# A gated convolution block on one core: five of TensorE's convolution tiles as three half-length filters, with their surroundings reordered

## The chip, the core and the metric

The kernel runs on one core of one Trainium2 chip. Time is device microseconds from start to end of one execution. The kernel before takes 1095.86 us, the median of 3 runs (1095.54 to 1095.91). Besides the times there is one profiled execution, from which all rows in this document are taken unless another kernel is named. Engines are PE (TensorE), PEld (its weight loads), DVE (VectorE), ACT (ScalarE), POOL (GpSimd) and SP (SyncE, which issues nearly all DMAs). L802 is line 802 of the kernel.

## What is computed

One layer of a decoder on 256 tokens of width 2048, in float32. A condition vector gives six modulation vectors; the mixer is a gated causal depthwise convolution with 31 taps, between two matrix products and followed by a layer norm; then comes an MLP of width 8192.

```python
mod = silu(c) @ mod_w + mod_b
sh1, sc1, g1, sh2, sc2, g2 = split(mod, 6)
h = rms_norm(x, norm1_g) * (1 + sc1) + sh1
a, gt = split(h @ conv_w_in + conv_b_in, 2)
u = a * sigmoid(gt)
u = depthwise_conv(u, dw_w, left padding 30) + dw_b     # 31 taps, each channel by itself
y = silu(layer_norm(u, ln_g, ln_b)) @ w_out + b_out
x = x + (1 + g1) * y
h = rms_norm(x, norm2_g) * (1 + sc2) + sh2
x = x + (1 + g2) * (square(relu(h @ mlp_w1)) @ mlp_w2)
```

## The kernel before

Activations lie with channels on partitions: 2048 channels are 16 tiles of 128 partitions x 256 tokens. Weights come as 1 MB blocks through seven "raw" buffers. Each is split into a high part (ScalarE, L209) and a low part (L213, on VectorE or GpSimd), and products are made of three reduced-precision matmuls.

The program is a list of jobs. Jobs 0 to 7 (the first half of the input product) run together at the start, at the pace of the DMAs. The loop then takes job 8 to 15 ("in", one tile of `a` and `gt` each), eight "out" jobs, and 64 "up" and "down" jobs. An in-job has 64 or 96 matmuls (L238, L239; job 15 merged, L234 to L236). Its result is added up on VectorE (L537, `evac`) and gated: ScalarE takes the sigmoid (L817), VectorE multiplies (L819, `gate`) and so writes u of the tile. The results of in-jobs and of TensorE's convolution tiles go in turn through two PSUM buffers called "mm"; the gate reads the buffer in place.

The 16 convolution tiles are shared out:

- Eight on VectorE (2, 3, 4, 5, 6, 8, 11, 13): 31 multiply-adds each ("taps", L670 to L676), two tiles interleaved, and a join (L679). `ADVANCE[n]` says how many taps are put into the program behind the gate of job n; the rest comes in job 14.
- One on GpSimd (tile 7): ScalarE multiplies (L703), GpSimd sums (L705), seven taps a job, `POOL_TAPS`.
- Seven on TensorE (0, 1, 9, 10, 12, 14, 15), `pe_conv`, L802. Partitions carry 32 channels x 4 neighbouring taps: `copy_wide` makes from u four shifted copies of 32 partitions, for each of four groups of channels (16 copies of 32x284, on ScalarE, L779; for tile 15 half on VectorE, L777). `make_diag` spreads the taps over diagonals of 32x32 (GpSimd, L787). A tile is then 8 matmuls for each of four groups, of 32 output columns and 256 tokens, side by side in the array. `CONV_AT` puts tile 0 behind job 9, 1 behind 10, 9 behind 11, 10 behind 12, 12 behind 14, 14 behind 15; `COPY_AT` puts the copies a job ahead. The result is evacuated by ScalarE (L810), or by VectorE for tiles 14 and 15.

Between jobs TensorE also computes modulation rows (`mod_chunk`, L328, 16 to 20 matmuls of 32 columns; `mod_finish`, L375, folds a finished group) and sums for the layer norm. `find_shift` (L428) takes the mean of two finished tiles; it is subtracted from every tile (`add_shift`, L741) so that the sums of squares stay exact. `stats` (L480 on ScalarE, L747 on TensorE) sums finished tiles and their squares by 32 columns: tiles 0 to 3 and 4 to 7 in job 14's turn, 8 to 11 behind tile 14. One modulation column ("col", a dot product of 2048 elements on VectorE, `mod_col`, L408) is taken in job 15's turn. Tile 15 is convolved last; then the layer norm follows.

What sets the order: each engine runs its instructions in order; a scheduler orders them by priority when the program is built, `urgent()` raises one, and `tc.issue_after` keeps one instruction behind another. Engines wait for each other by semaphores, and for a buffer until its last reader is done.

## Time and profile before

| | |
|---|---|
| median of 3 runs | 1095.86 us |
| profiled execution, its time | 1095.74 us |
| its span, first to last instruction | 1093.8 us |
| granted TensorE clock, mean | 0.997 |
| start, paced by DMAs | 0 to 123 us |
| in-jobs 8 to 15 with convolution | 137 to 283 us |
| layer norm, out-jobs, MLP | 283 to 1093 us |

A profile row gives the engine, line and operation, the tile written and the tiles read (out<-in), shapes and count. In groups, the figures are busy us and mean ns, then idle time of the engine just before and who ended it. In timelines and the chain, they are start and duration in us; operations of an engine overlap at their edges, so the step from one start to the next is some 0.09 us shorter than a duration. "x64" means that so many in a row were merged. In the row by stretches each engine has its busy us and instruction count.

### The profile page before, as it was taken

The page shows a single profiled execution, that of the slowest core. Times are in us where ns is not written, and L with a number is a line of the kernel's source. Part 1 is how long each engine was busy: PE and PEld are TensorE (multiplying, and loading weights), DVE is VectorE, ACT ScalarE, POOL GpSimd, SP SyncE. Part 2 cuts the span into 40 slices and gives each one's busy share as a digit, 9 for nine tenths or more (in the row PEclk, how much of TensorE's full clock was granted, in tenths as well). Part 3 has the DMA queues.
Part 4 walks back from the last instruction along what each step waited for, and adds up shares of the span by engine and source line. Part 5 has one row for each costly group of instructions (what it writes and reads, how often), then busy time and mean ns, then how long its engine had stood idle before and what let it go on. Part 6 is the DMA issues. An engine that isn't in the chain of part 4 may idle for free.

```text
span 1093.8 us, 15366 instructions
## 1 busy us (share of the span) xinstructions
PE 1075.9 (98%) x5970; PEld 889.9 (81%) x5970; DVE 748.5 (68%) x1019; ACT 520.1 (48%) x706; POOL 217.4 (20%) x149
## 2 busy tenths in 40 slices
PE   6999999999999999999999999999999999999998
PEld 3877876768699988888888888888888888888887
DVE  5777889997667877768855677545566665565653
ACT  4111398677675686444444444333444333444431
POOL 0000169989599251000000000000000000000000
PEclk8999999999999999999999999999999999999999
DMA  9999997995999967899977889657888877788611
GB/s 384 420 420 420 416 416 288 391 371 216 375 393 403 372 248 253 265 296 341 419 266 206 253 258 318 235 144 290 248 242 237 225 214 214 230 251 235 214 66 39
DMA packets 142314, 314.20 MB, mean 287 GB/s; under 512 B 87585, under 2 KB 105505, under 8 KB 107297
## 3 DMA queue, kind: packets, MB, share of 16 engines
q1 hardware_dynamic: 142096, 313.10, 81.6%
q8 instruction: 47, 0.77, 0.3%
q14 instruction: 25, 0.20, 0.0%
q10 hardware_dynamic: 146, 0.13, 0.0%
HBM read 301.13 MB, written 12.07 MB: 286 GB/s over the span
## 4 chain that ended last, share of the span: by engine, by line
PE 86%; DMA 10%; DVE 3%; ACT 1%; issue 0%; SPq 0%; ACTq 0%
PE mm L276 20%; PE mm L275 20%; PE mm L277 20%; DMA raw<-mod_c 9%; PE mm L238 6%; PE mm L239 3%; PE acc L235 2%; PE acc L234 2%; PE acc L236 2%; PE row L328 2%; PE mm L802 2%; DVE raw L408 1%; DMA x<-x 1%; DVE wide L777 1%; PE mm L234 0%; PE mm L236 0%
## 5 line engine op out<-in xcount | busy, mean ns | idle before, releaser
L209 ACT ACTIVATE hi<-raw 128x1024 fp32r<-128x1024 f32 x320 | 335.7, 1058 | 357.4 <-PE mm L277 328.3
L213 DVE TENSOR_TENSOR lo<-raw,hi 128x1024 fp32r<-128x1024 f32 x257 | 312.3, 1220 | 182.7 <-ACT hi L209 180.9
L276 PE MATMUL mm<-lo,u 128*128 128x512 f32 x496 | 193.0, 389 | 0.0
L275 PE MATMUL mm<-hi,u 128*128 128x512 f32 x496 | 193.0, 389 | 0.0
L277 PE MATMUL mm<-hi,u 128*128 128x512 f32 x496 | 192.9, 389 | 0.0
L277 PE MATMUL mm<-hi,hl 128*128 128x512 f32 x480 | 186.7, 389 | 0.0
L276 PE MATMUL mm<-lo,hl 128*128 128x512 f32 x480 | 186.7, 389 | 0.0
L275 PE MATMUL mm<-hi,hl 128*128 128x512 f32 x480 | 186.7, 389 | 0.0
L213 POOL TENSOR_TENSOR lo<-raw,hi 128x1024 fp32r<-128x1024 f32 x63 | 156.2, 2506 | 33.4 <-ACT hi L209 33.3
L408 DVE SCALAR_TENSOR_TENSOR raw<-raw,cond 128x2048 f32<-128x2048 f32 x50 | 117.8, 2358 | 40.5 <-DMA raw<-mod_c 40.5
L277 PEld LDWEIGHTS mm<-hi,u 128*128 128x128 f32 x496 | 93.1, 188 | 19.3
L276 PEld LDWEIGHTS mm<-lo,u 128*128 128x128 f32 x496 | 93.1, 188 | 19.1
L275 PEld LDWEIGHTS mm<-hi,u 128*128 128x128 f32 x496 | 93.1, 188 | 19.0
L277 PEld LDWEIGHTS mm<-hi,hl 128*128 128x128 f32 x480 | 90.1, 188 | 18.7
L275 PEld LDWEIGHTS mm<-hi,hl 128*128 128x128 f32 x480 | 90.1, 188 | 18.7
L276 PEld LDWEIGHTS mm<-lo,hl 128*128 128x128 f32 x480 | 90.1, 188 | 18.7
L676 DVE SCALAR_TENSOR_TENSOR acc<-u,v,acc 128x256 f32<-128x256 f32 x224 | 95.8, 488 | 1.8
L238 PE MATMUL mm<-hl,hi 128*128 128x512 f32 x224 | 80.3, 402 | 0.0
L580 PE MATMUL mm<-two,first 128*128 128x256 f32 x240 | 56.7, 390 | 8.9 <-ACT two L638 8.9
L234 PE MATMUL acc<-hl,hi 128*128 128x256 f32 x224 | 63.4, 283 | 0.0
L235 PE MATMUL acc<-hl,hi 128*128 128x256 f32 x224 | 63.4, 283 | 0.0
L236 PE MATMUL acc<-hl,lo 128*128 128x256 f32 x224 | 63.4, 283 | 0.0
(218 smaller groups left out, 1286.8 us busy)
## 6 DMA issues: line engine op xcount, KB each, us to landing
raw<-w SPq DMA_DIRECT2D x128, 1024.0 KB, 5.5
raw<-mod_c SPq DMA_DIRECT2D x62, 1024.0 KB, 11.3
raw<-mod_r SPq DMA_DIRECT2D x32, 1024.0 KB, 8.7
raw<-w_in SPq DMA_DIRECT2D x16, 1024.0 KB, 11.2
raw<-w_out SPq DMA_DIRECT2D x16, 1024.0 KB, 7.9
first<-w_first SPq DMA_DIRECT2D x15, 1024.0 KB, 19.8
flat<-two SPq DMA_DIRECT2D x30, 256.0 KB, 2.6
two<-flat SPq DMA_DIRECT2D x120, 64.0 KB, 4.4
```

Of the source, the lines that this page charges most:

```text
L209: state["w_hi"] = nc.scalar.activation(hi, w[:, ks, :], AF.Copy).ins
L213: end = by.tensor_tensor(lo, w[:, ks, :], hi.bitcast(F32), op=ALU.subtract)
L234: nc.tensor.matmul(out_p, w, m[:, 0:T], start=begin, stop=False)
L235: nc.tensor.matmul(out_p, w, m[:, T : 2 * T], start=False, stop=False)
L236: state["mm_end"] = nc.tensor.matmul(out_p, lo[:, k % HALF, :], m[:, 0:T], start=False, stop=end)
L238: nc.tensor.matmul(p[:, c, :], hi[:, k % HALF, :], m, start=(k == 0), stop=(k == KT - 1))
L275: nc.tensor.matmul(p, p_hi, hi, start=begin, stop=False)
L276: nc.tensor.matmul(p, p_hi, lo, start=False, stop=False)
L277: nc.tensor.matmul(p, p_lo, hi, start=False, stop=end)
L408: nc.vector.scalar_tensor_tensor(w, w, 1.0, cb, op0=ALU.mult, op1=ALU.mult, accum_out=acc)
L580: step = nc.tensor.matmul(held[n][:, c, :], w[:, 2 * n + c, :], h, start=k == 0 and c == 0, stop=k == KT - 1, skip_group_check=True)
L676: nc.vector.scalar_tensor_tensor(out, s, w, acc, op0=ALU.mult, op1=ALU.add)
```

## The change

Tiles 0, 1, 9, 10 and 12 (`FAST`) are convolved otherwise; 14 and 15 (`PLAIN`) as before. With even and odd samples of u and even and odd taps, both halves of the output come from three filters of 16 taps on 128 samples: the even taps on the sum of two neighbouring phases (needed by both), and two differences of taps, each on one phase. So:

- `copy_phases`: the 16 copies per tile now hold the two phases one after the other, 32 x (2 x 140), from every second sample of u.
- `add_phases`: VectorE adds the two phases (128x560), a buffer "added" of its own, behind the gate of the job before.
- `fast_conv`: 3 parts x 4 x 4 groups = 48 matmuls of 32 columns and 128 samples in place of 32 of 256. ScalarE evacuates the shared part with the bias (128x128), VectorE adds it to the two others into every second sample of the tile.
- `make_diag`: 48 in place of 32 diagonals for these tiles, one buffer in place of two (tile 14 has its own). Once ahead of the loop GpSimd subtracts the filters from each other (128x5x32).

Around it: `find_shift` moves from behind tile 1 to between job 11's matmuls and tile 9 and its two column sums stand together. `mod_finish` of an in-job waits for the end of that job's matmuls, and is not called again behind the rows. `stats` of tiles 0 to 3 moves behind the rows of job 13, that of 4 to 7 behind tile 12. The modulation column comes ahead of the last shift in the program, and that shift (tile 12) reads the SBUF copy. `ADVANCE` falls by 18 taps in jobs 9 to 13. For tile 15 VectorE makes six of the copies, ScalarE ten. u has eight buffers in place of nine, "rest" one in place of two, the partial products of tile 7 use mu and mu2, and the padding on the right side is smaller.

As built, the matmuls of jobs 9 to 14 have nothing between them; VectorE's stream holds add_phases one to four taps behind the gates of tiles 8 to 11 and 13; GpSimd's holds the diag of tiles 1, 9 and 10 between the sums of tile 7; and the modulation column stands between the gates of tiles 13 and 14.

```diff
 FIRST = 4
-PE_TILES = (0, 1, 9, 10, 12, 14, 15)
 CONV_AT = {9: (0,), 10: (1,), 11: (9,), 12: (10,), 14: (12,), 15: (14,)}
+FAST = (0, 1, 9, 10, 12)
+PLAIN = (14, 15)
+HT = T // 2
+PHASE = HT + 12
 POOL_TILE = 7
 POOL_TAPS = {8: 2, 9: 7, 10: 7, 11: 7, 12: 7}
-ADVANCE = {7: 41, 8: 10, 9: 44, 10: 47, 11: 39, 12: 34, 13: 24, 14: 99}
+ADVANCE = {7: 41, 8: 10, 9: 42, 10: 43, 11: 36, 12: 32, 13: 17, 14: 99}
 SHIFT = 2
+SHIFT_AT = 9
 COPY_AT = {8: 0, 9: 1, 10: 9, 11: 10, 13: 12}
-PADDING = 752
+PADDING = 672
 UNSHIFTED = 7
...
     nc.scalar.dma_start(v[:, 0:soon], vec[:, 0:soon])
-    dwq_sb = const.tile([P, 32 * len(PE_TILES)], F32, name="dwq_sb")
+    dwq_sb = const.tile([P, 48 * len(FAST) + 32 * len(PLAIN)], F32, name="dwq_sb")
 
...
         for i, s in enumerate(tiles):
-            nc.tensor.matmul(
-                p, ones, s, start=first and i == 0, stop=last and i == len(tiles) - 1
-            )
+            end = nc.tensor.matmul(p, ones, s, start=first and i == 0, stop=last and i == len(tiles) - 1).ins
+        return end
 
...
     last_mm(hl[HALF - 1][:, 1, :], ((hi_a, lo_a), (hi_b, lo_b)))
+    f = dwq_sb[:, 0 : 48 * len(FAST)].rearrange("p (t a b) -> p t a b", t=len(FAST), a=3)
+    with urgent():
+        nc.gpsimd.tensor_tensor(
+            f[:, :, 1:3, :], f[:, :, 1:3, :], f[:, :, 0:1, :].to_broadcast([P, len(FAST), 2, 16]), op=ALU.subtract
+        )
     start_scope.__exit__(None, None, None)
...
 
+    mu, mu2 = [cvp.tile([P, T], F32, name=name) for name in ("mu", "mu2")]
+
     def cv(k):
...
     u = {}
-    ubufs += [cp.tile([P, PAD + T + 1], F32, name=f"u{i}") for i in range(EARLY_U, 9)]
+    ubufs += [cp.tile([P, PAD + T + 1], F32, name=f"u{i}") for i in range(EARLY_U, 8)]
     for ub in ubufs[EARLY_U:]:
...
         acc = ps.tile([P, 2, T], F32, name="acc", bufs=2)
-        rest = cp.tile([P, T], F32, name="rest", bufs=2)
+        rest = cp.tile([P, T], F32, name="rest", bufs=1)
         for j in range(TAPS):
...
 
-    on_dve = [ct for ct in range(KT) if ct not in PE_TILES and ct != POOL_TILE]
+    on_dve = [ct for ct in range(KT) if ct not in FAST + PLAIN and ct != POOL_TILE]
     taken_taps = iter(range(1, TAPS))
...
         slots = [cvs[3][:, m, :] for m in range(4)] + [cv(11)]
-        slots += [cp.tile([P, T], F32, name="part", bufs=2) for _ in range(n - len(slots))]
+        slots += [mu, mu2]
         with urgent(), tc.issue_after(state["sg"].ins), tc.issue_after(state["pool"]):
...
         p = state["small"][:, 0:T]
-        column_sum(p, [cv(k) for k in range(SHIFT)])
+        end = column_sum(p, [cv(k) for k in range(SHIFT)])
         state["shift"] = cp.tile([P, T], F32, name="shift", bufs=1)
...
             nc.scalar.activation(dst, p, AF.Copy, scale=-1.0 / (SHIFT * P))
+        return end
 
...
 
+    added = {}
+
+    def copy_phases(ct):
+        wides[ct] = cp.tile([P, 4, 2, PHASE], F32, name="wide", bufs=2)
+        for q in range(4):
+            for g in range(4):
+                src = u[ct][32 * g : 32 * g + 32, 2 * q : 2 * q + 2 * PHASE].rearrange("p (x s) -> p s x", s=2)
+                nc.scalar.activation(wides[ct][32 * q : 32 * q + 32, g, :, :], src, AF.Copy)
+
+    def add_phases(ct):
+        added[ct] = cp.tile([P, 4, PHASE], F32, name="added", bufs=1)
+        nc.vector.tensor_tensor(added[ct], wides[ct][:, :, 0, :], wides[ct][:, :, 1, :], op=ALU.add)
+
     def copy_wide(ct, both=True):
+        if ct in FAST:
+            return copy_phases(ct)
         wides[ct] = cp.tile([P, 4, T + 28], F32, name="wide", bufs=2)
...
                 src = u[ct][32 * g : 32 * g + 32, q : q + T + 28]
-                if both and g % 2:
+                if both and g % 2 and q:
                     nc.vector.tensor_copy(dst, src)
...
     def make_diag(ct):
-        diags[ct] = cp.tile([P, 32, 32], F32, name="diag", bufs=2)
-        at = PE_TILES.index(ct)
+        fast = ct in FAST
+        n, at = (48, 48 * FAST.index(ct)) if fast else (32, 48 * len(FAST) + 32 * PLAIN.index(ct))
+        name = "diag14" if ct == PLAIN[0] else "diag"
+        whole = cp.tile([P, 32 if ct == PLAIN[0] else 48, 32], F32, name=name, bufs=1)
+        diags[ct] = whole[:, 0:n, :]
         with tc.issue_after(state["pool"]):
...
                 diags[ct],
-                col("same", 0, 32)[:, None, :].to_broadcast([P, 32, 32]),
-                dwq_sb[:, 32 * at : 32 * at + 32][:, :, None].to_broadcast([P, 32, 32]),
+                col("same", 0, 32)[:, None, :].to_broadcast([P, n, 32]),
+                dwq_sb[:, at : at + n][:, :, None].to_broadcast([P, n, 32]),
                 op=ALU.mult,
+            )
+
+    def fast_conv(ct):
+        wide, diag, total = wides.pop(ct), diags.pop(ct), added.pop(ct)
+        p = ps.tile([P, 2, 2 * T], F32, name="mm", bufs=2)[:, 0, :]
+        for part in (2, 1, 0):
+            for m in range(4):
+                for g in range(4):
+                    src = total[:, g, :] if part == 0 else wide[:, g, part % 2, :]
+                    at = HT * part
+                    state["conv_end"] = nc.tensor.matmul(
+                        p[32 * g : 32 * g + 32, at : at + HT], diag[:, 16 * part + 4 * g + m, :],
+                        src[:, 4 * m : 4 * m + HT], start=m == 0, stop=m == 3,
+                    )
+        with urgent():
+            shared = two()[:, 0, 0:HT]
+            nc.scalar.activation(shared, p[:, 0:HT], AF.Identity, bias=col("dwb", ct))
+            nc.vector.tensor_tensor(
+                cv(ct).rearrange("p (x s) -> p s x", s=2), p[:, HT : 3 * HT].rearrange("p (s x) -> p s x", s=2),
+                shared[:, None, :].to_broadcast([P, 2, HT]), op=ALU.add,
             )
...
     def mix(ct):
-        pe_conv(ct)
-        if ct == SHIFT - 1:
-            find_shift()
+        with tc.issue_after(find_shift()) if ct == SHIFT_AT else ExitStack():
+            (fast_conv if ct in FAST else pe_conv)(ct)
 
...
             splits(jobs[n + 1])
+        for ct in CONV_AT.get(n, ()):
+            if ct in FAST:
+                with tc.issue_after(state["gated"]):
+                    add_phases(ct)
         if n in COPY_AT:
...
                 mm(p, c, job + (c,), hl, merged=kind == "out")
-        mod_finish()
+        with tc.issue_after(state["mm_end"].ins) if kind == "in" else ExitStack():
+            mod_finish()
         if kind == "in":
...
             if n == KT - 1:
-                state["e_end"] = add_shift(cvs[3][:, 0:1, :], 1)
                 for key, w in taken:
                     mod_col(key[1], w)
+                state["e_end"] = nc.vector.tensor_tensor(cv(12), cv(12), state["shift"], op=ALU.add).ins
             for ct in CONV_AT.get(n, ()):
...
                     state["rows_end"] = state["row_end"].ins
-            if rows:
-                mod_finish()
             with tc.issue_after(state["gated"]):
                 advance(ADVANCE.get(n, 0))
-            if n == KT - 2:
-                with tc.issue_after(state["mm_end"].ins):
-                    for b in range(2):
-                        stats(b)
+            if n in (KT - 3, KT - 2):
+                with tc.issue_after(state["row_end" if n == KT - 3 else "conv_end"].ins):
+                    stats(n - KT + 3)
+                state["rows_end"] = state["stats_end"].ins
             if n < KT - 1:
...
             with urgent():
-                mu = cvp.tile([P, T], F32, name="mu")
-                mu2 = cvp.tile([P, T], F32, name="mu2")
                 factor = ps.tile([P, 512], F32, name="small", bufs=1)
...
     taps[:TAPS] = np.asarray(conv_dw_w)[0]
-    dwq = taps.reshape(8, 4, KT, 4, 32).transpose(1, 4, 2, 3, 0).reshape(P, KT, 32)[:, list(PE_TILES)]
-    dwq = np.ascontiguousarray(dwq.reshape(P, 32 * len(PE_TILES)))
+    def in_groups(a, n):
+        return a.reshape(n, 4, KT, 4, 32).transpose(1, 4, 2, 3, 0).reshape(P, KT, 4 * n)
+
+    even, odd = taps[0::2], taps[1::2]
+    ahead = np.concatenate([np.zeros((1, D), np.float32), odd[:-1]])
+    fast = np.stack([in_groups(a, 4)[:, list(FAST)] for a in (even, odd, ahead)], axis=2).reshape(P, -1)
+    dwq = np.concatenate([fast, in_groups(taps, 8)[:, list(PLAIN)].reshape(P, -1)], axis=1)
+    dwq = np.ascontiguousarray(dwq)
     pick = np.tile(np.eye(32, 4, dtype=np.float32), (4, 1))
```

## The prediction

> **What bounds the kernel now.** First TensorE's forty slices on the page, a group of its costliest (used below: one modulation column on VectorE, 2358 ns), and one stretch of the convolution stage in busy us by engine (TensorE, its weight loads, VectorE, ScalarE, GpSimd), clock and DMA.
>
> ```profile
> PE   6999999999999999999999999999999999999998
> ...
> L408 DVE SCALAR_TENSOR_TENSOR raw<-raw,cond 128x2048 f32<-128x2048 f32 x50 | 117.8, 2358 | 40.5 <-DMA raw<-mod_c 40.5
> ...
> 200.00:220.00 20.00, 20.00 (x177) 13.79 (x176) 20.00 (x55) 9.32 (x16) 19.53 (x14) 1.00 1.00 405
> ```
>
> TensorE is never idle for a slice after the start, at a clock of 1.00, so whatever it saves in the convolution stage shortens the run, unless it then waits. But in that stage VectorE is at 20.00 of 20 us and GpSimd at 19.53. The chain of waits in order of time shows TensorE's side: the in-jobs, and between them the convolution tiles (64 instructions each) and row matmuls.
>
> ```profile
> 169.16 0.43 PE mm L238
> 170.42 0.24 PE mm L238
> ...
> 180.67 3.59 PE mm L802 x64
> 184.26 0.63 PE small L428 x2
> 184.89 3.57 PE row L328 x32
> 188.46 0.43 PE mm L238
> ...
> 208.27 0.43 PE mm L238
> ...
> 227.57 0.43 PE mm L238
> ...
> 252.44 3.59 PE mm L802 x64
> 256.02 1.28 PE small L747 x20
> 257.31 0.32 PE mm L234
> ...
> 278.79 3.76 PE acc L802 x61
> ...
> 392.80 3.63 PE row L343 x128
> ```
>
> In-jobs 10, 11, 12, 13 and 15 begin at 169.1, 188.5, 208.3, 227.6 and 257.3. A job's matmuls take 11.5 us (169.16 to 180.67). Two "mm" buffers alternate between jobs and tiles, so each of these starts needs the gate of the job before (L819) to have read its buffer. Hence VectorE's timeline, the gates of tiles 9 to 15 and what stands around them:
>
> ```profile
> 167.31 0.48 DVE L819 SCALAR_TENSOR_TENSOR u<-mm,v,two 128x256 f32<-128x256 f32 x1 [0.54 <-ACT two L817]
> 167.71 10.27 DVE L676 SCALAR_TENSOR_TENSOR acc<-u,v,acc 128x256 f32<-128x256 f32 x26
> ...
> 184.54 0.69 DVE L537 TENSOR_TENSOR mm<-mm,two 128x512 f32<-128x512 f32 x1
> ...
> 186.05 0.48 DVE L819 SCALAR_TENSOR_TENSOR u<-mm,v,two 128x256 f32<-128x256 f32 x1
> ...
> 205.37 0.49 DVE L819 SCALAR_TENSOR_TENSOR u<-mm,v,two 128x256 f32<-128x256 f32 x1
> ...
> 224.89 0.48 DVE L819 SCALAR_TENSOR_TENSOR u<-mm,v,two 128x256 f32<-128x256 f32 x1
> ...
> 242.68 0.48 DVE L819 SCALAR_TENSOR_TENSOR u<-mm,v,two 128x256 f32<-128x256 f32 x1 [0.55 <-ACT two L817]
> ...
> 255.51 0.48 DVE L819 SCALAR_TENSOR_TENSOR u<-mm,v,two 128x256 f32<-128x256 f32 x1
> 255.90 5.73 DVE L676 SCALAR_TENSOR_TENSOR acc<-u,v,acc 128x256 f32<-128x256 f32 x11
> ...
> 266.73 3.52 DVE L408 SCALAR_TENSOR_TENSOR raw<-raw,cond 128x2048 f32<-128x2048 f32 x1
> ...
> 271.55 0.48 DVE L819 SCALAR_TENSOR_TENSOR u<-mm,v,two 128x256 f32<-128x256 f32 x1 [1.30 <-ACT two L817]
> 272.07 7.00 DVE L777 COPY wide<-u 32x284 f32<-32x284 f32 x8
> ```
>
> Job 10's matmuls end at 180.67, yet VectorE takes up the result at 184.54: it is 3.9 us behind, on conv taps. Its gates end only 1.3 (167.8 against 169.1), 2.0, 2.4, 2.3 and 1.4 us before TensorE starts the next job. TensorE is the bound by about 2 us; VectorE is next.
>
> **What TensorE saves.** The changed tile is 48 matmuls of 128 columns, 96 instructions. The row with their form (128x32 weights, 128 columns) is L343 above: 3.63/128 = 28.4 ns. So 96 x 28.4 = 2.72 us against 3.59: 0.87 each, 4.35 for five. [...]
>
> Regrouping: job 11 runs from 188.46 with one column-sum matmul in its middle; two beside each other and beside a tile save one re-entry, the difference of a first matmul's 0.43 and the usual 0.24. Three such places, with mod_finish and the sums inside job 15: 0.2 each, 0.6. All told TensorE needs 5.0 us less. The copies for tile 15 (272.07) shrink from eight on VectorE to six.
>
> **What VectorE gets.** Per fast tile two operations: add_phases, 128x560, two SBUF inputs; and the closing add, 128x256 from PSUM, 0.34 from one start to the next (below, as L1030 by size). ADVANCE takes taps out ahead of gates (2, 4, 3, 2, 7 of them), at 10.27/26 = 0.395 a tap between two tiles, 5.73/11 = 0.52 when one tile runs alone. Nothing removes a tap: they move to the last job. The price of add_phases hangs on GpSimd:
>
> ```profile
> 326.11 2.36 DVE L224 TENSOR_TENSOR u<-two,u 128x512 fp32r<-128x512 f32 x1 [0.65 <-ACT u L221]
> 330.88 0.69 DVE L1030 TENSOR_TENSOR x<-acc,x 128x512 f32<-128x512 f32 x1 [2.41 <-ACT acc L1029]
> 346.23 2.63 DVE L224 TENSOR_TENSOR u<-two,u 128x512 fp32r<-128x512 f32 x1 [4.02 <-ACT u L221]
> 367.44 0.72 DVE L224 TENSOR_TENSOR u<-two,u 128x512 fp32r<-128x512 f32 x1
> ...
> 323.14 7.59 POOL L213 TENSOR_TENSOR lo<-raw,hi 128x1024 fp32r<-128x1024 f32 x3
> 343.53 4.78 POOL L213 TENSOR_TENSOR lo<-raw,hi 128x1024 fp32r<-128x1024 f32 x2
> ```
>
> L224 takes 0.72 us while GpSimd is idle (367.44), but begun at 346.23 it ends at 348.86, 0.55 after GpSimd's subtraction (343.53 + 4.78 = 348.31). An operation with two SBUF inputs waits until GpSimd's current one is over, then runs; one with a PSUM input does not (L1030, 0.69). So add_phases costs 0.7 (0.64 step x 560/512) if GpSimd is free, and 0.7 + 2.4 if it has just begun a subtraction. GpSimd's own round:
>
> ```profile
> 179.72 9.45 POOL L213 TENSOR_TENSOR lo<-raw,hi 128x1024 fp32r<-128x1024 f32 x4
> 189.14 1.91 POOL L787 TENSOR_TENSOR diag<-v,dwq_sb 128x1024 f32<-128x1024 f32 x1
> 191.01 4.00 POOL L705 TENSOR_TENSOR cv<-cv,cv 128x256 f32<-128x256 f32 x5
> ...
> 213.58 9.50 POOL L213 TENSOR_TENSOR lo<-raw,hi 128x1024 fp32r<-128x1024 f32 x4
> ...
> 245.18 9.46 POOL L213 TENSOR_TENSOR lo<-raw,hi 128x1024 fp32r<-128x1024 f32 x4
> ```
>
> Four subtractions of 2.36, a diag that grows with 48/32 from 1.91 to 2.87, seven sums of 0.8: 17.9 us, always busy. The mean rest of the current operation is (9.45 x 1.18 + 2.87 x 1.43 + 5.6 x 0.4)/17.9 = 0.98. I take add_phases at 1.65, between its ends 0.7 and 3.1. The round itself grows by 1 us and by the adds it lets in, but job 13's weights begin at 213.58 and are wanted at 227.6: 14 us of cover, of which three diags and three adds use 5. The subtraction of filters ahead of the loop (160 elements) is under one 0.8 us sum, in GpSimd's wait for the first weights; its dwq load, 152 for 112 KB, is 0.1 us at the 405 GB/s above.
>
> ScalarE: sixteen phase copies per tile in place of sixteen wide ones, and a 128-column evacuation for a 256-column one.
>
> ```profile
> 154.44 7.19 ACT L779 ACTIVATE wide<-u 32x284 f32<-32x284 f32 x16
> ```
>
> No row shows every second element read. I take 0.45 a copy (7.19/16); the other end is double, 0.9. [...] With eight instead of nine u buffers, gates 8 and 9 reuse tiles 0 and 1 after their copies, the later of which end at 161.6 for a gate at 167.3: nothing; without that 5.7 us cover the gate would wait. The second buffers of diag and rest are gone: a diag is written in GpSimd's turn, 9.45 us of subtractions after the tile before it began, and a tile takes 2.7; rest is written and joined on one engine in order. Nothing either.
>
> **The gates, worked forward** in the built order of instructions, starts of L819. Gate 9 waits on ScalarE in both: 167.8. To gate 10, before 18.74 (186.05 - 167.31): four taps fewer (-1.57), a lone tap now paired (-0.13), +1.65 +0.34: 19.0, so 186.85. TensorE, 0.87 earlier at job 10, would need 19.3 (169.16 to 188.46) less 0.87 for the tile and 0.63 for the sums that leave this place, and be ready at 186.1; the gate ends at 187.25. To gate 11, before 19.32: five taps fewer (-1.96), a join traded for a closing add, +1.65: 205.85; TensorE, begun at 187.3, needs the 19.8 of before (188.46 to 208.27) less 0.87 and 0.2 and is ready at 206.0; the gate ends at 206.25. To gate 12, before 19.52: one tap and a pairing less (-0.5), a join more, half the shift-add left for later (-0.9), +2.0: 20.4, so 226.25, ending 226.65, with TensorE ready at 206.3 + 19.3 - 1.07 = 224.5. Job 13 begins at 226.7, before 227.57: of four tiles' 3.5 us and 0.4 of regrouping 0.9 is left. Gate 13 waits for ScalarE's copies at the closing add: 243.8, which delays nobody, since job 14 needs no gate.
>
> To gate 14 the modulation column (L408) now comes first: it was behind cv 12 at 266.73. Before 12.83; the add 1.65, the column 2.36 + 0.95 for GpSimd, four taps fewer (-2.0), 0.5 of idle time filled: 15.3, so 259.1. Its raw buffer comes free some 17 us sooner, and one load behind it on SP's queue goes earlier; no load is waited for there. Queued behind the column are gate 14 and so job 15: TensorE is ready at 226.7 + 29.7 (227.57 to 257.31) - 0.87 + 0.77 (twelve of its sums' 1.28/20 moved in) = 256.3 and begins at 259.5, 2.2 later than before. Job 15, rid of those twelve and a re-entry (-1.0), ends 1.2 late. Between gates 14 and 15 stand 22 lone taps (11.4), a closing add that waits for sixteen copies and one evacuation on ScalarE (259.5 + 16 x 0.45 + 0.4 = 267.1), and a shift with two SBUF inputs (0.34 + 1.0): gate 15 at 274.8, not 271.55. Then a tap and six copies, which take turns with GpSimd's last subtractions as the eight did: 275.2 + 6/8 of 7.00 = 280.4, not 278.79. Tile 15 starts there: **+1.6 us**. Behind it the code is the same and TensorE full, so this stays.
>
> The profiled run took 1095.74 around its span of 1093.8; the median is 1095.86. Sum: 1095.74 + 1.6 = 1097.3; on the median 1097.5. I say **1097.4**.
>
> **Rivals.** (a) The gates come in time and TensorE's 5.0 us stay: 1090.8. For it: every matmul is certain. Against it: even without the waits of add 10, add 12 and the column (0.95 each) gate 14 starts at 256.2, gate 15 (1.0 less for the shift) at 270.9, and ten copies on ScalarE end at 275.9 or later: tile 15 is some 2.8 us early, not 5. 12%. (b) GpSimd becomes the bound. Job 15 uses its second column half first, whose weights are the third subtraction of the round at 245.18: ready at 252.3, wanted at 257.3, 5 us of cover. Five diags at 1.0, five adds at 0.7 and the column at 2.36 that now falls into this round make 10.9 us, less GpSimd's idle time between rounds; from 5 us on job 15 waits for GpSimd, and with the 22 taps behind it, +3 to +5: 1099.8. For it: 19.53 of 20; against: TensorE is itself held back by the gates. 26%. (c) The short filters do not shorten: 57 ns per instruction as in L802, 5.5 us a tile, +9: 1105; or ScalarE's copies cost double, 7 us a job on an engine that all gates pass through: +8. L343 speaks against the first. 5%.
>
> **How the numbers follow.** Forecast (VectorE's gates pace, the gain is given back) 57%, its own range -2.8 (all adds 0.7) to +3.5 (half of them at 3.1, GpSimd's subtraction just begun): 1093.1 to 1099.4. A measurement tells 0.2% from no change, 2.2 us: 1093.7 to 1098.1. Of the forecast 6 points lie below, 43 within, 8 above; (a) is faster, (b) slower but for 2, (c) slower: 18%, 45%, 37%. Leaving out (a)'s better half, (c) and the tails, 1092.9 to 1100.3.
>
> **What would show it.** A fast tile of about 2.7 us in TensorE's rows; add_phases between 0.7 and 3.1; TensorE's idle time ahead of jobs 11, 13 and 15, ended by L819's gate; gate 15 after 274. Wrong: no such idle time and tile 15 before 275 (a), or idle ended by GpSimd's subtraction (b).

## The result and the profile after

| | before | changed |
|---|---|---|
| median, fastest to slowest | 1095.81 us (1095.54 to 1096.11, 6 runs) | 1103.52 us (1101.60 to 1105.01, 6 runs) |
| ratio, 95% interval | | 1.0069 [1.0056, 1.0082] |
| profiled execution, span, clock | 1095.74 us, 1093.8 us, 0.997 | 1104.61 us, 1102.8 us, 0.992 |

The changed kernel is 7.7 us slower, outside the predicted range, and its times spread by 3.4 us, those of the kernel before by 0.6. First the page of the changed kernel: TensorE's busy tenths and its granted clock in forty slices of 27.6 us, then the stretches of 20 us (columns as in the prediction: TensorE, its weight loads, VectorE, ScalarE, GpSimd, clock, DMA).

```profile
PE   7999999979999999999999999999999999999998
...
PEclk8999999998999999999999999999999999999999
```

```profile
220.00:240.00 20.00, 16.50 (x178) 11.42 (x178) 19.08 (x52) 13.68 (x29) 14.45 (x13) 0.91 0.98 398
240.00:260.00 20.00, 15.50 (x93) 11.04 (x92) 16.81 (x34) 7.29 (x9) 20.00 (x8) 0.83 0.82 308
```

Behind the first slice the kernel before has a 9 in every slice but the last; here one has a 7 (220 to 248 us), and the clock an 8 in the next. In the two stretches TensorE stands still for 8.0 us, and its granted clock falls to 0.91 and 0.83; before, it was busy without a break there, at 1.00. The chain of waits of the changed kernel, in order of time (start, us, what), shows both places:

```profile
220.34 2.80 PE mm L831 x96
223.14 3.46 issue
226.60 5.34 PE row L332 x32
231.94 0.43 PE mm L242
...
246.36 0.48 DVE u L868
246.84 0.40 DVE acc L686
247.24 1.26 DVE added L792
...
249.35 0.40 DVE acc L684
249.79 1.93 PE small L758 x16
251.73 0.73 PE mm L242
...
264.22 2.76 PE mm L831 x96
```

Job 13 (the `mm L242` at 231.94) and job 14 (251.73) are late, each behind a pause. A fast tile itself is as short as forecast, 2.76 us. The second pause is read backwards: the sums of tiles 0 to 3 (L758) start when the first shifted tap of tile 13 on VectorE (L684) is done, and in front of that tap stand two other taps, add_phases (L792), a tap (L686), and gate 13 (L868). TensorE's longest wait in the convolution stage names the same releaser (us in total, times, longest):

```profile
PE small L758 <- DVE acc L684: 4.5, 1, 4.5
```

The sums write columns 0 to 255 of the PSUM buffer "small", the tap reads the shift in its columns 256 to 511; as the kernel is built, a write waits for the last reader of the whole buffer. The first pause has no releaser in the chain ("issue"). VectorE's timeline around it shows it:

```profile
225.55 0.69 DVE L540 TENSOR_TENSOR mm<-mm,two 128x512 f32<-128x512 f32 x1
226.15 0.35 DVE L370 TENSOR_TENSOR modc<-row,v 128x4 f32<-128x4 f32 x4
...
227.14 0.48 DVE L868 SCALAR_TENSOR_TENSOR u<-mm,v,two 128x256 f32<-128x256 f32 x1
```

The rows behind tile 10 (L332) write the one PSUM buffer "row". L370 reads the folded group out of it, and it now stands behind 24 taps and the result of job 12 (L540), because the fold has moved behind the matmuls of job 12. The rows start at 226.60, when L370 is done. Before, L366 (the same line) ran at 216.4, in the middle of the job.

How the 9.0 us of span add up, from the starts on TensorE's timeline:

| start of | before | changed | difference | what came in |
|---|---|---|---|---|
| job 12 | 208.20 | 207.99 | -0.2 | |
| job 13 | 227.50 | 231.87 | +4.4 | pause 3.5; rows take 5.3, not 3.6; fast tile -0.9 |
| job 14 | 240.86 | 251.66 | +10.8 | pause 4.5; sums 1.9, of which 0.9 moved here |
| job 15 | 257.24 | 267.77 | +10.5 | job 14 12.5, not 11.5; fast tile -0.9; fewer sums |
| tile 14 | 270.11 | 279.48 | +9.4 | sums no longer inside job 15 |
| tile 15 | 278.79 | 287.75 | +9.0 | waits for the copies 0.8, not 1.3 |

Rows, sums and job 14 take longer because the clock is halved behind each pause. TensorE alone in stretches of 2 us (busy us and count, clock, DMA):

```profile
224.00:226.00 2.00, 0.00 (x0) 1.00 1.01 410
226.00:228.00 2.00, 1.40 (x9) 0.74 0.98 401
228.00:230.00 2.00, 2.00 (x16) 0.50 0.87 283
230.00:232.00 2.00, 2.00 (x17) 0.91 0.96 369
...
248.00:250.00 2.00, 0.21 (x4) 0.50 0.93 336
250.00:252.00 2.00, 2.00 (x17) 0.50 0.99 401
252.00:254.00 2.00, 2.00 (x7) 0.50 1.02 430
```

### The profile page after: what moved, and what is told of

Same layout as the page of the kernel before. It is cut to its first block, busy times and chain, and to the rows that moved or that the text cites. A ratio compares the mean times of both kernels' runs of the same rounds, so it can differ in the third digit from the quotient of the medians.

```text
span 1102.8 us, 15691 instructions
## 1 busy us (share of the span) xinstructions
PE 1076.7 (98%) x6130; PEld 895.4 (81%) x6130; DVE 754.0 (68%) x1027; ACT 522.0 (47%) x708; POOL 224.4 (20%) x148
## 4 chain that ended last, share of the span: by engine, by line
PE 78%; DMA 11%; DVE 6%; ACT 3%; issue 1%; POOL 0%; SPq 0%; DVEq 0%; POOLq 0%
PE mm L280 20%; PE mm L279 20%; PE mm L281 20%; DMA raw<-mod_c 7%; PE mm L242 4%; PE acc L239 2%; PE acc L238 2%; PE acc L240 2%; DVE acc L686 2%; DMA first<-w_first 2%; PE mm L243 2%; DMA raw<-mod_r 1%; DVE raw L412 1%; DMA raw<-w_in 1%; ACT wide L788 1%
## 5 line engine op out<-in xcount | busy, mean ns | idle before, releaser
L686 DVE SCALAR_TENSOR_TENSOR acc<-u,v,acc 128x256 f32<-128x256 f32 x224 | 95.6, 483 | 1.4
L242 PE MATMUL mm<-hl,hi 128*128 128x512 f32 x224 | 80.7, 404 | 0.8 <-DVE u L868 0.8
## 6 DMA issues: line engine op xcount, KB each, us to landing
raw<-w_in SPq DMA_DIRECT2D x16, 1024.0 KB, 10.2
```

What stands on the lines that cost most here:

```text
L242: nc.tensor.matmul(p[:, c, :], hi[:, k % HALF, :], m, start=(k == 0), stop=(k == KT - 1))
L686: nc.vector.scalar_tensor_tensor(out, s, w, acc, op0=ALU.mult, op1=ALU.add)
```

## The experiments

Each kernel was timed in five rounds, 4 to 11 executions, beside the kernel before, whose medians were 1095.66 to 1095.80. The intervals of e5, e13, e15 and e16 reach 1.000, no change; of the gains only those of e17 and e18, 0.2% and 0.1%, are clear of it.

| run | what | median us | ratio, 95% interval |
|---|---|---|---|
| e1 | changed, sums freed of the tap | 1100.37 | 1.0043 [1.0031, 1.0056] |
| e2 | changed, fold back | 1104.30 | 1.0075 [1.0062, 1.0088] |
| e3 | both | 1099.26 | 1.0035 [1.0021, 1.0048] |
| e4 | before, with the two moves alone | 1101.36 | 1.0045 [1.0032, 1.0057] |
| e5 | e3 without add_phases | 1095.67 | 1.0005 [0.9996, 1.0014] |
| e6 | changed, second pause filled | 1102.47 | 1.0054 [1.0041, 1.0066] |
| e7 | tiles 10 and 12 fast | 1100.76 | 1.0046 [1.0033, 1.0059] |
| e8 | tiles 9, 10 and 12 fast | 1107.39 | 1.0106 [1.0092, 1.0119] |
| e9 | e8 with other padding | 1098.84 | 1.0028 [1.0017, 1.0039] |
| e10 | tile 12 fast, sums together | 1105.75 | 1.0091 [1.0076, 1.0107] |
| e11 | before, sums together, six copies | 1103.68 | 1.0071 [1.0058, 1.0084] |
| e12 | five fast, sums together | 1106.19 | 1.0096 [1.0082, 1.0110] |
| e13 | tile 12 fast | 1094.79 | 0.9992 [0.9983, 1.0000] |
| e14 | five fast, sums and fold back | 1098.79 | 1.0028 [1.0018, 1.0039] |
| e15 | before, six copies | 1095.46 | 0.9997 [0.9988, 1.0006] |
| e16 | tiles 10 and 12 fast, repaired | 1094.79 | 0.9991 [0.9982, 1.0000] |
| e17 | e13 with four copies | 1093.67 | 0.9983 [0.9973, 0.9992] |
| e18 | before, four copies | 1094.45 | 0.9988 [0.9979, 0.9998] |

### The two pauses: e1 to e4

e1 lets one tap read the shift elsewhere:

```diff
+            by = state["shift"] if ct == 13 else state["small"][:, T : 2 * T]
-            nc.vector.scalar_tensor_tensor(out, s, w, state["small"][:, T : 2 * T], op0=ALU.mult, op1=ALU.add)
+            nc.vector.scalar_tensor_tensor(out, s, w, by, op0=ALU.mult, op1=ALU.add)
```

> The changed kernel (1103.5 us), but the first shifted tap of tile 13 on VectorE reads the copy of the shift in SBUF, so that the sums of tiles 0 to 3, which now stand ahead of job 14, no longer wait for it. Theory W (two new waits of TensorE for VectorE, and the halved clock behind each): job 14 begins about 5.3 us sooner (246.4, not 251.7), at full clock, and tile 15 5.5 us sooner: 1098.0. Rival G (the gates behind add_phases and the closing adds set the pace, as in the prediction): the time stays within 1 us of 1103.5. Rival F (the filters themselves cost the time): 1103.5.

e2 puts the fold back:

```diff
-        with tc.issue_after(state["mm_end"].ins) if kind == "in" else ExitStack():
-            mod_finish()
+        mod_finish()
...
+            if rows:
+                mod_finish()
```

> The changed kernel, but with mod_finish where it was before, so that the fold of the modulation group stands in the middle of job 12 and not behind its matmuls. Theory W: the rows behind tile 10 follow it at once (223.1, not 226.6) at full clock; job 13 then waits for gate 12 alone and begins at 228.7, not 231.9; all later work 3.2 us sooner: 1100.3. Rival G: gate 12 sets the start of job 13 in any case, 1103.5. Rival F: 1103.5.

> Both edits at once: the sums of tiles 0 to 3 freed of VectorE's tap, and mod_finish where it was. Theory W: the two add up, 1095.0 to 1095.5, no clock below 0.95 in any stretch of 10 us from 150 to 290. Rival G with the prediction's gates: 1097.4. Rival F: over 1100.

e4 makes the two moves in the kernel before, the reverse of e2's diff and:

```diff
-            if n == KT - 2:
-                with tc.issue_after(state["mm_end"].ins):
-                    for b in range(2):
-                        stats(b)
+            if n in (KT - 3, KT - 2):
+                with tc.issue_after(state["row_end" if n == KT - 3 else "conv_end"].ins):
+                    stats(n - KT + 3)
+                state["rows_end"] = state["stats_end"].ins
```

> The kernel before, without any fast tile, with only the two moves: mod_finish behind the matmuls of an in-job, and the sums of tiles 0 to 3 ahead of job 14, of 4 to 7 behind tile 12. Theory W: the sums wait for the first shifted tap of tile 13 at 244.8 in place of 240.9, TensorE idles 4 us and runs 2 us at half clock: 1101, with the clock below 0.95 around 250; the fold costs under 1 us here, since gate 12 is on time. Rival G and rival F: no fast tile, so 1095.8.

e4 came out as theory W has it: without a fast tile the moves cost 5.6 us on the median (3.2 to 5.8 in its five executions). One line of e4's view of TensorE's waits (us in total, times, longest), and the clock there, in stretches of 5 us:

```profile
PE small L747 <- DVE acc L674: 3.9, 1, 3.9
```

```profile
240.00:245.00 5.00, 1.13 (x16) 0.84 0.89 339
245.00:250.00 5.00, 5.00 (x26) 0.50 0.94 372
```

e1 confirms the wait: job 14 began at 246.1 and the pause was gone. But it gained 3.1 us and not 5.5. The edit had a price that I had not put in: a tap with both inputs in SBUF waited for GpSimd's current operation. VectorE's timeline of e1, and ahead of it GpSimd's operation of that moment:

```profile
247.89 3.28 POOL L817 TENSOR_TENSOR diag<-v,dwq_sb 128x1536 f32<-128x1536 f32 x1
...
249.29 2.17 DVE L685 SCALAR_TENSOR_TENSOR acc<-u,v,shift 128x256 f32<-128x256 f32 x1
...
251.77 4.10 DVE L412 SCALAR_TENSOR_TENSOR raw<-raw,cond 128x2048 f32<-128x2048 f32 x1
```

The diag ends at 251.17, the tap at 251.46: 2.17 us in place of the 0.47 that it took with the shift in PSUM, and the column behind it 4.10, not 2.46: gate 14 was late, and job 15 waited 2.1 us for it.

e2 is the miss that teaches most. The rows went at once, job 13 began 2.6 us sooner, and the time did not fall (+0.8 us on the median, within the spread). In its place TensorE waited 2.7 us for gate 12, which halved the clock again (job 13 took 12.9 us, not 11.5), so that gate 13 came only 1.3 sooner. Then:

```profile
245.06 0.48 DVE L868 SCALAR_TENSOR_TENSOR u<-mm,v,two 128x256 f32<-128x256 f32 x1 [1.56 <-ACT two L866]
...
245.85 2.81 DVE L792 TENSOR_TENSOR added<-wide 128x560 f32<-128x560 f32 x1
...
249.42 0.48 DVE L684 SCALAR_TENSOR_TENSOR acc<-u,v,small 128x256 f32<-128x256 f32 x1
```

The add met GpSimd at another moment and took 2.81 us, not 1.35, so that the tap that releases the sums ended at 249.9, as before. TensorE's wait for it grew from 4.5 to 6.0 us. The first pause is thus hidden behind the second one: with the second out (e1 to e3) the fold is worth 1.1 us. e3 has neither of these two pauses. It is still 3.5 us behind the kernel before and some 4 us over theory W's figure; TensorE waits 2.7 us for gate 12 and 2.7 us for gate 14 there, and job 15 runs partly at half the clock (0.50).

### What is left: e5 and e14

e5 takes add_phases out of e3:

```diff
-                    add_phases(ct)
...
-                    src = total[:, g, :] if part == 0 else wide[:, g, part % 2, :]
+                    src = wide[:, g, part % 2, :]
```

> The kernel of e3 (both waits removed, 1099.3 us), but add_phases is left out: the part shared by both halves is computed from one phase alone, so five sums of two phases are missing; TensorE's work is the same. Theory V (what is left of the loss in e3 is VectorE's: it is busy without a break from gate 9 to gate 15 and its adds of 0.7 to 2.4 us push every gate): the five adds are 7.6 us, the gates 10 to 14 come 1.5 to 5 us sooner, TensorE's idle time ahead of jobs 13 and 15 (2.7 us each) shrinks to under 1, tile 15 begins at 278.5 or sooner: 1094 to 1096. Rival P (a fixed loss of the filters on TensorE or of the copies on ScalarE): 1099.

It fell by 3.6 us on the median, as theory V says; TensorE, with the same matmuls, had waited for VectorE's adds. Six of its eleven times lie from 1095.41 to 1095.67, five from 1096.83 to 1097.54, 1.7 to 2.4 us below e3's median; why there are two groups is open. Nor do the adds explain everything: without them the kernel should have TensorE's 5 us to gain and is only level with the kernel before. In e5 TensorE waits 5.5 us in all from 130 to 292 us, for copies (2.1), gates (2.0) and loads (1.4). e14 is the change with everything mended, sums and fold in their old places, and with the copies for tile 14 put behind tile 12's evacuation on ScalarE, so that VectorE's closing add does not wait for them:

```diff
-                if i >= KT - 2:
-                    copy_wide(i, i == KT - 1)
+                if i == KT - 1:
+                    copy_wide(i)
...
+                if n == KT - 2:
+                    with urgent(), tc.issue_after(state["shared"]):
+                        copy_wide(14, False)
```

(`state["shared"]` is ScalarE's evacuation in fast_conv.)

> All five fast tiles, sums and fold where the kernel before has them, the copies for tile 14 behind the evacuation of tile 12: neither of the two waits, no dearer tap. Theory V (VectorE is full from gate 9 to gate 15): job 13 still begins near 229.4, gate 14 comes at 258.7 (e3: 260.8), tile 15 at 279 (e3: 282.1): 1096 to 1097, not faster than the kernel before. Rival (a) of the prediction, TensorE keeps its 5 us once the waits are gone: 1091. Rival P (a fixed loss in the filters): 1099.

1098.79, some 2 us over what theory V had said and far from rival (a). It is rival P's figure (1099, a fixed loss in the filters), but not for P's reason: a fast tile takes 2.8 us of TensorE here too (before, 3.7), and TensorE loses the time in waits, 8.5 us of them where the kernel before has 1.3. The largest part, 5.4 us, are gates (L868):

```profile
PE mm L242 <- DVE u L868: 3.6, 2, 2.8
PE mm L238 <- DVE u L868: 1.8, 1, 1.8
PE row L332 <- DMA raw<-mod_r: 1.6, 2, 1.3
PE acc L851 <- DVE wide L803: 1.3, 1, 1.3
```

and VectorE is close to full through all of it, in stretches of 20 us (columns as above):

```profile
210.00:230.00 20.00, 17.20 (x194) 13.03 (x193) 20.00 (x52) 8.91 (x16) 18.78 (x14) 1.00 0.98 390
230.00:250.00 20.00, 20.00 (x119) 15.99 (x118) 18.69 (x43) 16.16 (x27) 15.04 (x11) 1.00 0.88 344
250.00:270.00 20.00, 18.12 (x222) 15.62 (x221) 19.30 (x34) 13.24 (x25) 20.00 (x9) 1.00 0.70 265
```

In the kernel before VectorE had 15.03 of 20 us to do from 250 to 270, and 19.96 and 18.33 in the two stretches ahead. That was nearly all the room there was, and the adds and the taps taken out ahead of the gates have filled it.

### The clock: e6

```diff
+FILL = 8
...
+            p = early_p if n == KT - 2 else ps.tile([P, 2, 2 * T], F32, name="mm", bufs=2)
...
+                    early_p = ps.tile([P, 2, 2 * T], F32, name="mm", bufs=2)
+                    with tc.issue_after(end):
+                        for _ in range(FILL):
+                            end = nc.tensor.matmul(early_p[:, 0, 0:T], ones, cv(0), start=True, stop=True).ins
```

> The changed kernel (1103.5 us) with eight matmuls more, of no use to the result, in TensorE's wait ahead of the sums of tiles 0 to 3 (3.8 of its 4.5 us), written to the buffer that job 14 overwrites. The wait itself stays as long. Theory K (idle time of some 3 us halves the granted clock for some 4 us): no drop between 246 and 256, the sums take 0.9 and not 1.9 us and job 14 11.4 and not 12.4, so job 14 ends 2 us sooner: 1101.5. Rival (the clock follows something else, or the time behind the wait is lost for another reason): 1103.5.

The clock did what theory K says. TensorE of e6 in stretches of 4 us, the same in which the changed kernel has 0.68, 0.50 and 0.97:

```profile
246.00:250.00 4.00, 3.58 (x30) 1.00 1.02 430
250.00:254.00 4.00, 4.00 (x24) 1.00 1.01 428
254.00:258.00 4.00, 4.00 (x24) 1.00 0.95 330
```

The sums took 1.0 us and job 14 11.5. On the median the useless work in the wait gained 1.05 us, half of what was expected and less than either kernel's times spread, so the gain in time is not shown; the clock is. Its times fall in two groups, 1100.35 and 1100.36 against 1102.47 to 1102.66. In the profiled one (1100.35) the first pause, 2.76 us there, did not halve the clock either; none of the other group was profiled.

### How many fast tiles: e7 to e9

e7 and e8 are the changed kernel with fewer fast tiles, and sums, fold, shift and column in their old places:

```diff
-FAST = (0, 1, 9, 10, 12)
-PLAIN = (14, 15)
+FAST = (10, 12)
+PLAIN = (0, 1, 9, 14, 15)
-ADVANCE = {7: 41, 8: 10, 9: 42, 10: 43, 11: 36, 12: 32, 13: 17, 14: 99}
+ADVANCE = {7: 41, 8: 10, 9: 44, 10: 47, 11: 39, 12: 31, 13: 20, 14: 99}
```

(e8: `FAST = (9, 10, 12)`, and 46, 38, 30, 18 taps behind jobs 10 to 13.)

> Only tiles 10 and 12 by short filters, the other five as before; sums, fold, shift and column where they were before, 7 taps fewer ahead of the gates (3 in job 12, 4 in job 13). Theory V: VectorE has room for these two adds (it waits 3.8 us ahead of the last shift in the kernel before, and its gates 13 and 14 wait for ScalarE): TensorE keeps the 0.87 us of both tiles up to job 14, one of them up to tile 15, whose copies are two fewer on VectorE: 1094.6, faster than both kernels. Rival P: each fast tile costs, 1096.5 or more.

> Tiles 9, 10 and 12 by short filters, the rest as in e7 with 16 taps fewer ahead of the gates than in the kernel before. Theory V: the add behind gate 10 lies where VectorE has no room; gates 11 and 12 come 0.5 to 1 us late: 1094.5 to 1096, not better than e7. Rival P: 1097 or more; the prediction's rival (a), every tile's 0.87 us is kept: 1093.7.

Both were far slower, and mostly for a reason that no theory named. Behind the layer norm, where nothing was changed, e8 lost 8 us. The groups of the products with u2, for the kernel before and e8 (busy us, mean ns):

```profile
L276 PE MATMUL mm<-lo,u 128*128 128x512 f32 x496 | 193.0, 389 | 0.0
L275 PE MATMUL mm<-hi,u 128*128 128x512 f32 x496 | 193.0, 389 | 0.0
L277 PE MATMUL mm<-hi,u 128*128 128x512 f32 x496 | 192.9, 389 | 0.0
```

```profile
L279 PE MATMUL mm<-hi,u 128*128 128x512 f32 x496 | 195.7, 395 | 0.0
L281 PE MATMUL mm<-hi,u 128*128 128x512 f32 x496 | 195.7, 395 | 0.0
L280 PE MATMUL mm<-lo,u 128*128 128x512 f32 x496 | 195.7, 395 | 0.0
```

Three groups by 2.7 make 8.2 us. Their operands had moved: the filter tables take 224 columns in the kernel before, 304 in the changed one and 272 in e8, and the padding 752, 672 and 672. In the first two the sum is 976, in e8 it was 944. e9 changes one number:

```diff
-PADDING = 672
+PADDING = 704
```

> The kernel of e8 (tiles 9, 10 and 12 fast, 1107.4 us) with the padding at 704 columns in place of 672, so that padding and filter tables together take the 976 columns that they take in the kernel before and in the changed one. Theory S (in e8 the products with u2 take 395 and not 389 ns, 8.2 us in all, because of where their operands lie in SBUF): 389 ns again, 1107.4 - 8.2 = 1099.2. Rival (those products are slower for another reason): 1107.

1098.84, and the products took 389 ns again, one group of the three:

```profile
L280 PE MATMUL mm<-lo,u 128*128 128x512 f32 x496 | 193.0, 389 | 0.0
```

The change's smaller padding thus is not idle: with its own tables it keeps the sum at 976. In e7, at 928 columns, the stretch from tile 15 to the end of the span was 3.4 us longer than before (818.4 us from 280.14, against 815.0 from 278.79). What is left of e8, 3.1 us in e9, is mostly gates: jobs 12 and 13 waited 0.7 and 2.7 us. So e7 and e8 as they were run do not tell what two or three fast tiles are worth.

### Runs that did not tell: e10 to e12

> Only tile 12 by short filters, padding at 736 so that the 976 columns stay; all orders as in the kernel before, but the sums of tiles 0 to 7 stand together behind tile 12, the copies for tile 14 follow the evacuation of tile 12 on ScalarE, and VectorE makes six copies for tile 15. Theory V (VectorE has room for one add, behind gate 13): TensorE needs 0.87 less ahead of job 15 and one re-entry less in it, tile 15 begins 1 to 2 us sooner than 278.8: 1094.0. Rival: the add of up to 2.8 us delays gate 14, 1096 or more.

> The kernel before without any fast tile, with two of the side moves of e10: the sums of tiles 0 to 7 together behind tile 12, and six copies on VectorE for tile 15. If these moves alone carry what e10 gains: the same time as e10. By the rows, a re-entry of 0.2 to 0.3 and a copy round of 0.5 less: 1095.0 to 1095.5, so that 1 us or more of e10 would be the fast tile's.

> All five fast tiles, without either of the two waits and without the dearer tap of e3: sums of tiles 0 to 7 together behind tile 12, fold where it was before, the copies for tile 14 behind the evacuation of tile 12. Theory V: VectorE saves 1.3 us on the tap and some on the column before gate 14, job 15 begins near 259 (e3: 261.4), but VectorE stays full from gate 9 to gate 15 and the five adds keep the gates late: 1097, between the kernel before and e3. Rival (a) of the prediction, TensorE keeps its 5.0 us once the waits are gone: 1091.

All three have the sums of tiles 0 to 7 in one piece behind tile 12:

```diff
             if n == KT - 2:
-                with tc.issue_after(state["mm_end"].ins):
-                    for b in range(2):
-                        stats(b)
+                with tc.issue_after(state["conv_end"].ins):
+                    stats(0)
+                    stats(1)
+                state["rows_end"] = state["stats_end"].ins
```

and in all three that made a third pause; TensorE's one wait in e10:

```profile
PE small L758 <- ACT sq L483: 10.2, 1, 10.2
```

(e10 has tile 12 fast, e11 none, e12 all five; e10 and e12 have the copies for tile 14 as in e14.) The squares of tiles 4 to 7 stand on ScalarE behind the sixteen copies for tile 14. In e11 and e12 the wait was 7.4 and 8.4 us. The kernel before puts these sums into the middle of job 15, where the squares are ready; I had made the mistake of the change itself. About fast tiles these runs say nothing.

### One or two fast tiles: e13, e15 to e18

e13 has only tile 12 fast, everything else as before, but for ten taps fewer in `ADVANCE[13]`, the copies for tile 14 as in e14, and six copies; e16 adds tile 10.

```diff
-FAST = (0, 1, 9, 10, 12)
+FAST = (12,)
-PADDING = 672
+PADDING = 736
```

> Tile 12 alone by short filters, 976 columns of tables and padding kept, and now with the sums where the kernel before has them (in e10 they waited 10 us for ScalarE's squares behind sixteen copies); ten taps fewer ahead of gate 14; copies for tile 14 behind the evacuation of tile 12; six copies for tile 15. Theory V (room for one add behind gate 13): gate 14 at 255.5 in spite of an add of up to 3.1 us, job 15 begins at 256.3 (before 257.2), tile 15 at 277.2 (before 278.8): 1094.2. Rival: the add delays gate 14 or the sums wait in job 15, 1095.8 or more.

e15, the control, changes the kernel before in one line (e11 has it too):

```diff
-                if both and g % 2:
+                if both and g % 2 and q:
```

> The kernel before with six instead of eight of the copies for tile 15 on VectorE, nothing else. TensorE waits 1.26 us for the last of VectorE's copies there; VectorE needs 0.87 each, ScalarE 0.45: 1095.2 to 1095.5. If e13 gains no more than this, its fast tile brings nothing.

> Tiles 10 and 12 fast, sums and fold as before, 976 columns kept, two taps fewer ahead of gate 13 and ten ahead of gate 14, otherwise as e13. Theory V: gate 12 has no room for the add behind gate 11 (in e7 it came 1.0 us late), so tile 10 gains nothing and this is no better than e13: 1094.2 to 1095.5. Rival (a): 0.87 us better than e13.

e13 held its steps in the profiled execution, with an add that took 3.12 us: gate 14 at 255.0, job 15 at 255.9 (before 257.2), tile 15 at 277.3 (before 278.8). On the median it gains 0.9 us, 0.6 less than expected, the copies alone 0.2; neither interval excludes no change. The second tile brings nothing (e16, the same median). What TensorE then waited for most was VectorE's copies for tile 15, 1.0 us in both. So the last pair moves two more of them to ScalarE, with the fast tile (e17) and without it (e18):

```diff
-                if both and g % 2 and q:
+                if both and g % 2 and q > 1:
```

> The kernel of e13 (tile 12 fast, 1094.8 us) with four of the copies for tile 15 on VectorE and twelve on ScalarE, in place of six and ten. In e13 VectorE's six take 6.77 us beside GpSimd, ScalarE's ten 4.50, and TensorE waits 1.03 us for VectorE's last. Theory V: VectorE's four end near 275.3, ScalarE's twelve at 276.2, when TensorE has done the rows: tile 15 at 276.3, 1.0 sooner: 1093.8, faster than both kernels. Rival (the next wait takes its place at once): 1094.8.

> The kernel before with four copies for tile 15 on VectorE, no fast tile: the control of e17. The wait of 1.26 us for VectorE's copies goes, ScalarE's twelve end at 277.5, as TensorE is ready: 1094.6. Then the fast tile of e17 is worth 0.8 us.

Both came out within 0.2 us of the expectation. e17, at 1093.67, is faster than both kernels, by 2.1 us and 9.9 us. Of the 2.1 the copies make 1.3, and the fast tile 0.8, close to its 0.87 us on TensorE. The fast tile's share includes what goes with it (ten taps fewer ahead of gate 14, the copies for tile 14 put later); these were not timed apart. TensorE's waits of e17 from 130 to 292 us, all of them:

```profile
PE acc L851 <- ACT wide L805: 0.2, 1, 0.2
PE acc L851 <- DVE wide L803: 0.2, 1, 0.2
```

## Why the prediction was wrong, point by point

- **TensorE's saving.** Right. A fast tile took 2.76 us against 2.72 forecast, 28.8 ns an instruction (2.76/96) where L343's row has 28.4, and job 11 lost the column sum in its middle and a re-entry (11.4 us, not 11.9). Only the re-entry of mod_finish saved nothing: job 12 with its fold took 12.3 us in both kernels.
- **ScalarE's copies.** Right. Reading every second sample costs next to nothing, a median of 454 ns against 439 for the contiguous copies of the kernel before (the changed kernel's copies, min/median/max ns, first and last start):

```profile
L788 ACT ACTIVATE wide<-u x80: 436/454/478, 140.3 to 236.9; 32x280 f32<-32x280 f32 x80
```

- **add_phases.** Right, in size and in cause (min, median, max ns in the changed kernel; the mean is 1.51 us against 1.65 forecast; one add of e13 took 3.12 us). A small slip in its reading: GpSimd was not idle yet at 367.44, where L224 took 0.72; a sum of GpSimd ended at 367.61, so the operation alone is nearer 0.6, by this estimate.

```profile
L792 DVE TENSOR_TENSOR added<-wide x5: 735/1352/2381, 154.7 to 247.1; 128x560 f32<-128x560 f32 x5
```

- **The step that failed.** "Gate 13 waits for ScalarE's copies at the closing add: 243.8, which delays nobody, since job 14 needs no gate." Job 14 needs none, but the sums had been moved ahead of it, and the prediction counted them as matmuls (0.77 of the 1.28 us), not as writers of a buffer that VectorE reads behind gate 13. The wait was 4.5 us, and the clock behind it took 1.9 more. e1, which frees the sums, and e4, which makes the moves without a fast tile, show it.
- **The same fault once more.** mod_finish was entered under "regrouping", as a re-entry saved. That the rows behind it write the buffer which its last step on VectorE reads, and that this step now stands behind 24 taps, was missed: 3.5 us of waiting ahead of the rows. e2 shows the wait, and that it is hidden behind the pause of the sums; with that pause out, it is worth 1.1 us.
- **The clock.** Not forecast. It makes 1.7 us in the rows (5.3 against 3.6), 0.9 in the sums (1.9 against 1.0) and 1.0 in job 14 (12.5 against 11.5). e6 shows the last two going when the pause is filled.
- **The gates.** Sign and mechanism right, as far as e14 shows them, the size 1.5 us short, and the nearness of two gates in part luck. e14 has the change without the two pauses (and with the copies for tile 14 put later), and there the gates can be compared with the forecast; of the idle time that the prediction named, that ahead of jobs 13 and 15 is there, 2.8 and 1.8 us, ended by the gates; ahead of job 11 there is next to none (0.2):

| | forecast | changed | e14 |
|---|---|---|---|
| gate 10 | 186.85 | 187.67 | 187.6 |
| gate 11 | 205.85 | 207.35 | 207.2 |
| gate 12 | 226.25 | 227.14 | 228.7 |
| gate 13 | 243.8 | 246.36 | 244.3 |
| gate 14 | 259.1 | 267.02 | 259.4 |
| gate 15 | 274.8 | 281.86 | 274.6 |
| tile 15 | 280.4 | 287.75 | 281.9 |

  What was off: the forecast counts starts, but begins from gate 9 at 167.8, which in its own row is the end (167.31 + 0.48); gate 9 started at 168.4 in the changed kernel, 168.3 in e14. VectorE waited 4.0 us for ScalarE's evacuation ahead of three closing adds of the changed kernel; the sum had the two ahead of gates 13 and 15, not the 1.1 us for tile 0. Gate 12 of e14 is 2.4 us late. That gates 14 and 15 still lie within 0.3 us of the forecast is errors that cancel: the column took 4.6 us, not 3.3, and the shift 2.0, not 1.3, while the closing add of tile 12, for which the forecast had a wait, did not wait in e14. The six copies took 5.27 us in the changed kernel, as forecast (5.25), but 6.60 in e14.
- **The rivals.** (a), TensorE keeps its 5 us, is refuted by e14. (b), GpSimd as the bound, did not come: its sign, idle time of TensorE ended by GpSimd's subtraction, is in neither the changed kernel nor e14. GpSimd was full from 250 to 270 in e14 (20.00 of 20 us) but had room ahead of it (15.04 from 230 to 250); through the adds that wait for it, it does set part of VectorE's time. (c), longer filters or dearer copies, is refuted by the tile of 2.76 us and the copies of 454 ns. The prediction had no rival for a wait that the moves make, though the diff moves three things past VectorE's queue.
- **Behind tile 15.** Right: +9.0 us there and +9.0 in the span.

## What to carry to other kernels

When a step is moved, list the buffers that it writes and who reads them last, and look where that reader stands in its own engine's queue: if that engine is late, the moved step now waits for it. That a job needs no gate says nothing of the steps put in front of it. Work taken from the busiest engine pays only as far as the next engine has room; here VectorE had room for one add (tile 12; a second, for tile 10, brought nothing). One fast tile, with four copies handed to ScalarE, is 2.1 us faster than the kernel before, 1.3 of it by the copies; five fast tiles (e14) were 3.1 us slower. If a fix does not move the time, look for the same releaser behind the next wait before giving up the theory.

## What the runs showed of the hardware that was not expected

**Half the clock already came behind a pause of 2.45 us.** All pauses of more than 1.2 us between 150 and 292 us in the profiled executions of the changed kernel, e1 to e12 and e14, by the granted clock in stretches of 1 us behind them:

| pause | halved to 0.50 | not |
|---|---|---|
| 1.2 to 2.2 us | 0 | 11 |
| 2.4 to 2.8 us | 5 (2.45, 2.52, 2.66, 2.66, 2.68) | 3 (2.73, 2.76, 2.80) |
| 3.4 to 10.2 us | 8 | 0 |

Behind a pause the half clock lasted for some 3.3 us (e12) to 5.4 us (e4) of work, by the same stretches. Between 2.4 and 2.8 us the length does not decide: the clock stayed at 1.00 behind 2.80 us and fell to 0.50 behind 2.45. The times of some kernels with such a pause fall into groups 1.5 to 2 us apart (e6, above; e3 with 1099.01 to 1099.33 and 1100.76). That the clock makes the groups is not shown: only one execution of each was profiled, and e5 has two groups though the pauses of its profiled execution are 1.5 us at most.

**The padding alone moved a matmul's time by 1.5%.** Products with u2 took 395 ns at 944 columns of tables and padding (e8), 389 ns at 976 (e9, with 32 columns more padding); at 928 (e7) the stretch from tile 15 on was 3.4 us longer than before. Why was not tried.

**VectorE's operations with two SBUF inputs took their length from GpSimd's moment.** The same add took 0.73 (changed kernel) to 3.12 us (e13), and the same tap 0.47 from PSUM, 1.79 (e3) and 2.17 us (e1) from SBUF. What came on top was the rest of GpSimd's current operation: e1's tap ended 0.29 us behind the diag (251.46 against 251.17), and three of the changed kernel's five adds 0.60 to 0.62 us behind a subtraction (those that ended at 156.01, 191.02 and 247.90). That was up to 2.4 us for the add (3.12 - 0.73) and 1.7 us for the tap (2.17 - 0.47).
